# Four pairs of k instead of three by Strassen's products, in every second group of gates and ups

## The chip, the core and the metric

The kernel runs on one core of a Trainium2 chip. The metric is the time of one execution in device microseconds; the median of three runs is given, and beside it the profiler's record of one execution.

## What is computed

A decoder block for 256 positions of width 2048 in float32: a mixer (causal pooling and differential attention), and then a dense feed-forward part. The change lies in the feed-forward part alone:

```python
D_MODEL = 2048
D_FF = int(math.ceil(8 * D_MODEL / 3 / 256) * 256)   # 5632
...
hn = rms_norm(h, pre_ffn_norm[l])
ff = (jax.nn.silu(hn @ w_gate[l]) * (hn @ w_up[l])) @ w_down[l]
h = h + rms_norm(ff, post_ffn_norm[l])
```

## The kernel before

**Three matmuls for one product.** Every float32 operand is split in two parts: ScalarE copies it to a rounded part (named with h: `wh`, `rh`, `gh`), VectorE subtracts that from the operand and leaves the rest (named with l: `wl`, `rl`, `gl`). A product is then three matmuls: rounded by rounded, rest by rounded, rounded by rest. In `product` they stand in lines 768, 769 and 770; the first two read `wh`, the third is the first to read `wl`.

**Groups and pairs.** The 5632 columns of gate and up are 11 groups of 512. The first group is done apart. The other ten, c = 1 to 10, take gate and up together: k runs over 2048 rows in eight pairs (j = 0 to 7) of two blocks of 128 rows. For one pair there are four blocks of weights (two of k, by up and gate) and four blocks of h (two of k, by two halves of the positions). A plain pair multiplies them in 8 products, 24 matmuls of 128x512. A pair listed in `SK` takes Strassen's form (with Winograd's sums) of 7 products, 21 matmuls: three on single blocks of weights (`rh`, `rl`), and four on sums of blocks (`wh`, `wl` of the tile `T`). The sums of h for such a pair are the same for every group; `h_sums` makes them once, ahead of the ten groups, while the first group's ups run.

**What is done for one pair, q, and when.** `first_stage(q)` starts the two transfers of the four blocks into `raw` (three buffers in turn) and, in a Strassen pair, has VectorE make `T` (one buffer): one addition of 128x1024 and two of 128x512. `raw_stage(q)` splits three blocks into `rh` and `rl` (two buffers each) for a Strassen pair. `last_stage(q)` splits either `T` or `raw` into `wh` and `wl` (two buffers each), 128x2048. The loop over pairs runs `products(q)`, then `last_stage(q + 1)`, `first_stage(q + 2)` and `raw_stage(q + 2)`: while TensorE is at pair q, VectorE makes wl of the next pair, then T and rl of the one after it. Within a Strassen pair the order of products is 1, 3, 2 (on rh, rl: nine matmuls), then 7, 6, 4, 5 (on wh, wl). So its third matmul is the first to read `rl`, its twelfth the first to read `wl`.

**What sets the order.** Each of the three engines works its queue in the order written: `put` ties every matmul, copy and subtraction of this stage behind the one before it on its engine. Elsewhere a scheduler interleaves. Added to the pairs are the ends of the groups: behind pair 6 and behind pair 7 VectorE joins the products' sums (`u`, `sg`), behind pair 0 of the next group it multiplies gate and up (`gg`), and TensorE transposes the result (`g_part`).

Of the kernel before, what the change touches and what calls it, by code (L numbers as in the profile page):

```python
# [15 lines left out]
P = 128  # L16
# [13 lines left out]
H_GATE = {(0, 0): (0, 3), (0, 7): (1, 0), (0, 9): (1, 1), (0, 11): (1, 2), (1, 2): (1, 3)}  # L30
RING = 3
WINDOWS = (2, 4, 8, 16)
SK = (1, 3, 5)
CMB = 8


# [9 lines left out]
def block_kernel(ctx: ExitStack, tc: tile.TileContext, x, xT, pos, cols, rows, lamv, invf, invcnt,  # L46
# [4 lines left out]
    cp = ctx.enter_context(tc.tile_pool(name="cp", bufs=1))  # L51
# [8 lines left out]
    def nm(s):  # L60
        uid[0] += 1
        return f"{s}_{uid[0]}"

    def small(shape, dt=F32, tag="tiny", bufs=24):
        return tiny.tile(shape, dt, tag=tag, name=nm(tag), bufs=bufs)
# [20 lines left out]
    def load_after(dst, src):  # L86

        with tc.issue_after(latest[0]):
            sync.dma_start(dst, src)
# [51 lines left out]
    def gemm_a(srcs, a, nk, order=None, before=lambda i: None):  # L141
        ps = [bank(), bank()]
        for i, k, wh, wl in a_steps(srcs, order):
            before(i)
            for t in range(2):
                mm_a(ps, a, t, k, wh, wl, i == 0, i == nk - 1)
        return ps
# [127 lines left out]
    for k in range(NKD):  # L275
        n = 1 if k < 2 else 2
        i, j = k // 4, k % 4
# [5 lines left out]
        for m in range(2):  # L283
            raw, hi, lo = raws[m]
            c = slice(j % 2 * 512, (j % 2 + n) * 512)
# [3 lines left out]
        for m in range(2):  # L289
            raw, hi, lo = raws[m]  # L290
            if n == 1 or j % 2 == 0:
                c = slice(j % 2 * 512, (j % 2 + n) * 512)
                act.activation(hi[:, c], raw[:, c], AF.Copy)
                dve.tensor_tensor(lo[:, c], raw[:, c], hi[:, c].bitcast(F32), ALU.subtract)
            c = slice(j % 2 * 512, (j % 2 + 1) * 512)
# [237 lines left out]
    def closing(srcs_of, a, nk, gains, order, tail, parts, hook, done):  # L533

        sst = small([P, 2, 4], tag="sst", bufs=2)
        mg = {}

        def square(c, t, ps):
            j2 = cp.tile([P, 512], mybir.dt.bfloat16, tag="sqj", name=nm("sqj"), bufs=2)
            act.activation(j2, ps, AF.Square, accum_out=sst[:, t, c:c + 1])  # L540

        def gained(c, t, ps):
            mg[c, t] = mg_tile()
            dve.tensor_tensor(mg[c, t], ps, gain, ALU.mult)

        for c in range(4):
            if c == 1:
                act.activation(small([P, 1]), sst[:, 0, 0:1], AF.Sqrt)
            gain = cp.tile([P, 512], F32, tag="gain", name=nm("gain"), bufs=2)
            load_after(gain, gains[c * 512:(c + 1) * 512].partition_broadcast(P))  # L550
            if c < 3:
                ps = gemm_a(srcs_of(c), a, nk, order, lambda i: before_k[0](c, i))
                for t in range(2):
                    square(c, t, ps[t][:, :])
                    gained(c, t, ps[t][:, :])
        pre = small([P, 2])
        dve.tensor_reduce(pre, sst[:, :, 0:3], AX.X, ALU.add)
        pre2 = small([P, 2])
        dve.tensor_scalar(pre2, pre, 1.0 / D, EPS, ALU.mult, ALU.add)
        for t, ps in gemm_a_skew(srcs_of(3), a, nk, order, range(nk - tail, nk), parts, hook):  # L560
            square(3, t, ps[:, :])
            v = variance(sst[:, t, 3:4], 1.0 / D, pre2[:, t:t + 1])
            gained(3, t, ps[:, :])
            rs = rsqrt(v)
            for c in range(4):
                for z in (slice(0, 256), slice(256, 512)) if c == 0 and t == 1 else (slice(0, 512),):
                    dve.scalar_tensor_tensor(h_c(c, t)[:, z], mg[c, t][:, z], rs, h_c(c, t)[:, z], ALU.mult, ALU.add)
                    done(c, t, z)
# [31 lines left out]

    def h_stats(t):
        for c in range(4):
            j2 = cp.tile([P, 512], mybir.dt.bfloat16, tag="sqj", name=nm("sqj"), bufs=2)
            with tc.issue_after(behind_act[0]):
                act.activation(j2, h_c(c, t), AF.Square, accum_out=ss3[:, t, c:c + 1])
        ss3s = small([P, 1])
        dve.tensor_reduce(ss3s, ss3[:, t, :], AX.X, ALU.add)
        dve.tensor_copy(rstd3[:, t:t + 1], rsqrt(variance(ss3s, 1.0 / D)))
# [49 lines left out]
        sums_h[j], sums_l[j] = h, l  # L658


    h_at = dict(zip(range(2, 16, 4), SK))
    ps = gemm_a([w_u0[i] for i in range(4)], a_h, NKD, None, lambda i: h_sums(h_at[i]) if i in h_at else None)
    p_ring.close()
    ring2 = ctx.enter_context(tc.tile_pool(name="ring2", bufs=1, side="right", reuse_waits="tile"))
# [12 lines left out]
    def tt(out_, a, b, op):  # L677
        put("dve", lambda: dve.tensor_tensor(out_, a, b, op))  # L678
        return out_
# [37 lines left out]
    cmb = lambda name: ft.tile([P, 512], F32, tag="cmb", name=nm(name), bufs=CMB)  # L717

    NP = NKD // 2
    pairs = [(c, j) for c in range(1, NF // 4) for j in range(NP)]  # L720
    raws, sums, of_raw, of_sum = {}, {}, {}, {}

    def first_stage(q):

        if q >= len(pairs):
            return
        c, j = pairs[q]
        raws[q] = raw = blocks(w_gu[c - 1], j)
        if j in SK:
            sums[q] = s = part("T", 4, F32, 1)  # L730
            tt(s[:, 0:2], raw[:, 1:3], raw[:, 0:1].to_broadcast([P, 2, 512]), ALU.add)
            tt(s[:, 2], s[:, 0], raw[:, 2], ALU.add)
            tt(s[:, 3], s[:, 2], raw[:, 3], ALU.add)

    def raw_stage(q):

        if q < len(pairs) and pairs[q][1] in SK:
            rh = high(raws[q][:, 1:4], "rh")
            of_raw[q] = rh, low(raws[q][:, 1:4], rh, "rl")

# [20 lines left out]
    m, left, total, u = {}, {}, {}, {}  # L761
# [10 lines left out]
    def products(q):  # L772
        c, j = pairs[q]
        k1, k2 = 2 * j, 2 * j + 1
        if j == 0:
            m.update({1: bank(), 2: bank(), 3: bank(), 4: bank(), 6: bank2(), 8: bank2()})
            m[7] = psum_m.tile([P, 512], F32, tag="m7", name=nm("m7"), bufs=1)
            left.update({i: len(SK) + (2 * (NP - len(SK)) if i in (2, 3, 4) else 0) for i in range(1, 8)})
            left[8] = 2 * (NP - len(SK))
            total.update(left)  # L780
        wh, wl = of_sum[q]
        if j not in SK:
            for i, t, up in ((2, 0, 0), (4, 1, 0), (3, 0, 1), (8, 1, 1)):
                for k, b in ((k1, 1 - up), (k2, 3 - up)):
                    product(i, hh(k, t), wh[:, b], wl[:, b])
            return
        if j == SK[0]:
            m[5] = m5_bank()
        rh, rl = of_raw[q]
        form = lambda i: (sums_h[j][:, i], sums_l[j][:, i])  # L790
        product(1, hh(k1, 0), rh[:, 0], rl[:, 0])
        product(3, form(3), rh[:, 1], rl[:, 1])
        product(2, hh(k2, 0), rh[:, 2], rl[:, 2])
        product(7, form(1), wh[:, 1], wl[:, 1])
        product(6, form(2), wh[:, 2], wl[:, 2])
        product(4, hh(k2, 1), wh[:, 3], wl[:, 3])
        product(5, form(0), wh[:, 0], wl[:, 0])
# [5 lines left out]
    gg = [gated(ps[t][:, :], t) for t in range(2)]  # L803
    for q, (c, j) in enumerate(pairs):
        products(q)
        if j == SK[-1] + 1:
            u.update({n: cmb(f"u{n}") for n in (1, 2, 3, 4)})
            copy(u[1], m[1][:, :])
            tt(u[2], m[6][:, :], u[1], ALU.add)
            tt(u[3], m[7][:, :], u[2], ALU.add)  # L810
            last_stage(q + 1)
            tt(u[4], m[5][:, :], u[2], ALU.add)
            tt(u[2], m[5][:, :], u[3], ALU.add)
            first_stage(q + 2)
        elif j == NP - 1:
            last_stage(q + 1)
            sg = [cp.tile([P, 512], F32, tag="gain", name=nm("sg"), bufs=2) for _ in range(2)]
            for t, (i, n) in enumerate(((2, 1), (4, 3))):
                tt(sg[t], m[i][:, :], u[n], ALU.add)
                copy(sg[t], sg[t], AF.Silu, scale=rstd3[:, t:t + 1])  # L820
            first_stage(q + 2)
            for i, n in ((3, 4), (8, 2)):
                tt(u[n], m[i][:, :], u[n], ALU.subtract)
            raw_stage(q + 2)
            g_part(c - 1, gg, 0)
            if c == NF // 4 - 1:
                g_part(c - 1, gg, 1)
                g_split(0, gh0)
                gg = [gated(u[n], t) for t, n in enumerate((4, 2))]
        elif j == 0 and c > 1:  # L830
            last_stage(q + 1)
            new = [gated(u[n], t) for t, n in enumerate((4, 2))]
            first_stage(q + 2)
            raw_stage(q + 2)
            g_part(c - 2, gg, 1)
            gg = new
        else:
            last_stage(q + 1)
            first_stage(q + 2)
            raw_stage(q + 2)  # L840
# [40 lines left out]
    def mg_tile():  # L881
        n = len(mgs)
        if used[0] == n:
            three = part("rh" if n % 2 == 0 else "rl", 3, F32)
            mgs.extend(three[:, i] for i in range(3))
        used[0] += 1
        return mgs[used[0] - 1]
# [68 lines left out]
```

## Time and profile before

| | |
|---|---|
| median of three runs | 1024.69 us (1024.68 to 1025.0) |
| the profiled execution's own time | 1026.65 us |
| its span, first to last instruction | 1024.8 us |
| TensorE busy | 1012.2 us, 99% |
| VectorE busy | 735.5 us, 72% |
| ScalarE busy | 539.5 us, 53% |
| moved | 203.39 MB, 198 GB/s on the mean |

The profile gives busy times of each engine over the span, the same in 40 slices, the chain of work that ended last, followed back from the last instruction, and groups of like instructions. In a row of a timeline stand the start and the duration in us, the engine, the line of the kernel, the operation, output and inputs (buffer numbers left out), shapes, and in brackets the idle time of that engine just before it with what ended it. A window row gives, for a stretch of the span, its length, the busy time of TensorE's matmuls, of its weight loads, of VectorE, ScalarE and GpSimd, then TensorE's granted clock, the share of the DMA engines' time and GB/s. PE is TensorE, DVE is VectorE, ACT is ScalarE, SP the queue that starts the transfers. Matmuls are pipelined, so their rows overlap: the distance of starts is their price, not the duration.

### The profile page before, as it was taken

To read this page: it belongs to the slowest core of one execution; us is meant where nothing else is said; L and a number is where in the kernel's file an instruction comes from. 1 tells how busy PE (TensorE), PEld (TensorE's weight loads), DVE (VectorE), ACT (ScalarE), POOL (GpSimd) and SP (SyncE) were. 2 spreads that over 40 slices of the span, in tenths; PEclk is the share of its full clock that TensorE was granted. 3 is DMA by queue.
4 is the path that set the end of the run, shared out by engine and by line. 5 is a ranking of instruction groups with operands and counts; after the bars stand their busy time and mean duration, and the time that the engine had idled before them with its cause. 6 is when DMAs were issued, how large, how long until landed. Compare 5 with 4: busy or idle time off the path is not lost.

```text
span 1024.8 us, 12559 instructions
## 1 busy us (share of the span) xinstructions
PE 1012.2 (99%) x4787; PEld 841.7 (82%) x4787; DVE 735.5 (72%) x850; ACT 539.5 (53%) x643; POOL 28.4 (3%) x54
## 2 busy tenths in 40 slices
PE   9999999999999999999999999999999999999996
PEld 6889888988877888888888888888887888888885
DVE  6569755875677889898888988889887653454445
ACT  6666545654548555455454554645545553343332
POOL 0003300210000000000000000000000000000000
PEclk9999999999999999999999999999999999999999
DMA  9753555456774465555655556556565575556552
GB/s 337 284 191 131 180 186 177 151 169 217 237 255 135 165 228 192 199 201 194 206 197 195 202 185 205 206 201 200 174 211 189 196 287 198 191 196 216 181 189 82
DMA packets 57373, 203.39 MB, mean 198 GB/s; under 512 B 6880, under 2 KB 7520, under 8 KB 56544
## 3 DMA queue, kind: packets, MB, share of 16 engines
q1 hardware_dynamic: 57024, 202.44, 57.4%
q8 instruction: 37, 0.61, 0.2%
q14 instruction: 24, 0.20, 0.1%
q10 hardware_dynamic: 288, 0.15, 0.1%
HBM read 198.37 MB, written 4.19 MB: 198 GB/s over the span
## 4 chain that ended last, share of the span: by engine, by line
PE 98%; DVE 1%; DMA 0%; ACT 0%; issue 0%; DVEq 0%; SPq 0%; ACTq 0%
PE mm L136 16%; PE mm L137 16%; PE mm L135 16%; PE mm L768 9%; PE mm L769 9%; PE mm L770 9%; PE tr L770 3%; PE tr L769 3%; PE tr L768 3%; PE mm L174 2%; PE mm L175 2%; PE mm L176 2%; PE m L768 1%; PE m L769 1%; PE m L770 1%; PE m L692 1%
## 5 line engine op out<-in xcount | busy, mean ns | idle before, releaser
L100 DVE TENSOR_TENSOR wl<-raw,wh 128x1024 fp32r<-128x1024 f32 x88 | 104.7, 1222 | 107.6 <-ACT wh L99 107.6
L100 DVE TENSOR_TENSOR wlo<-raw,whi 128x1024 fp32r<-128x1024 f32 x89 | 110.5, 1241 | 61.9 <-ACT whi L99 56.5
L99 ACT ACTIVATE wh<-raw 128x1024 fp32r<-128x1024 f32 x88 | 89.3, 1052 | 122.4 <-PE mm L136 118.8
L678 DVE TENSOR_TENSOR wl<-raw,wh 128x2048 fp32r<-128x2048 f32 x50 | 114.6, 2292 | 44.0 <-ACT wh L674 43.7
L136 PE MATMUL mm<-wh,gl 128*128 128x512 f32 x352 | 137.3, 390 | 1.1 <-DVE gl L758 1.1
L674 ACT ACTIVATE wh<-raw 128x2048 fp32r<-128x2048 f32 x50 | 95.9, 1918 | 79.5 <-PE tr L769 56.4
L135 PE MATMUL mm<-wh,gh 128*128 128x512 f32 x352 | 134.9, 390 | 0.0
L137 PE MATMUL mm<-wl,gh 128*128 128x512 f32 x352 | 131.0, 389 | 0.0
L768 PE MATMUL mm<-wh,h 128*128 128x512 f32 x330 | 129.2, 392 | 0.0
L99 ACT ACTIVATE whi<-raw 128x1024 fp32r<-128x1024 f32 x89 | 94.0, 1056 | 65.7 <-PE mm L136 49.9
L769 PE MATMUL mm<-wh,h 128*128 128x512 f32 x330 | 128.5, 389 | 0.0
L770 PE MATMUL mm<-wl,h 128*128 128x512 f32 x330 | 128.4, 389 | 0.0
L674 ACT ACTIVATE wh<-T 128x2048 fp32r<-128x2048 f32 x30 | 57.6, 1920 | 73.8 <-DVE T L678 73.4
L136 PEld LDWEIGHTS mm<-wh,gl 128*128 128x128 f32 x352 | 66.1, 188 | 15.1 <-DVE gl L758 1.6
L137 PEld LDWEIGHTS mm<-wl,gh 128*128 128x128 f32 x352 | 66.1, 188 | 13.7
L135 PEld LDWEIGHTS mm<-wh,gh 128*128 128x128 f32 x352 | 66.0, 188 | 13.6
L678 DVE TENSOR_TENSOR wl<-T,wh 128x2048 fp32r<-128x2048 f32 x30 | 68.7, 2290 | 8.0 <-ACT wh L674 8.0
L770 PEld LDWEIGHTS mm<-wl,h 128*128 128x128 f32 x330 | 62.0, 188 | 12.9
L768 PEld LDWEIGHTS mm<-wh,h 128*128 128x128 f32 x330 | 62.0, 188 | 12.7
L769 PEld LDWEIGHTS mm<-wh,h 128*128 128x128 f32 x330 | 62.0, 188 | 12.5
L135 PE MATMUL mm<-whi,x 128*128 128x512 f32 x160 | 62.9, 395 | 0.6 <-ACT x L255 0.6
L136 PE MATMUL mm<-whi,x 128*128 128x512 f32 x160 | 62.8, 394 | 0.0
(246 smaller groups left out, 1941.3 us busy)
## 6 DMA issues: line engine op xcount, KB each, us to landing
raw<-in_w_gu SPq DMA_DIRECT2D x160, 512.0 KB, 4.2
raw<-in_w_down SPq DMA_DIRECT2D x88, 512.0 KB, 4.1
raw<-in_w_in SPq DMA_DIRECT2D x46, 512.0 KB, 3.8
raw<-in_w_out SPq DMA_DIRECT2D x32, 512.0 KB, 4.2
raw<-in_w_u SPq DMA_DIRECT2D x24, 512.0 KB, 3.7
raw<-in_w_g SPq DMA_DIRECT2D x8, 512.0 KB, 6.1
xn<-in_x SPq DMA_DIRECT2D x2, 1024.0 KB, 10.1
gain<-in_rows SPq DMA_DIRECT2D x8, 256.0 KB, 4.6
```

The costliest lines, as they stand in the source:

```text
L99: last_split[0] = act.activation(hi, raw, AF.Copy).ins
L100: (by or dve).tensor_tensor(lo, raw, hi.bitcast(F32), ALU.subtract)
L135: mm.matmul(ps[t][:, :], lhsT=a[0](k, t), rhs=wh, start=first, stop=False)
L136: mm.matmul(ps[t][:, :], lhsT=a[1](k, t), rhs=wh, start=False, stop=False)
L137: last_mm[0] = mm.matmul(ps[t][:, :], lhsT=a[0](k, t), rhs=wl, start=False, stop=last).ins
L174: mm.matmul(o, lhsT=wh, rhs=xh, start=st, stop=False)
L175: mm.matmul(o, lhsT=wh, rhs=xl, start=False, stop=False)
L674: put("act", lambda: act.activation(out_, in_, func, **kw))
L678: put("dve", lambda: dve.tensor_tensor(out_, a, b, op))
L768: put("mm", lambda: mm.matmul(o, lhsT=a[0], rhs=wh, start=first, stop=False))
L769: put("mm", lambda: mm.matmul(o, lhsT=a[1], rhs=wh, start=False, stop=False))
L770: put("mm", lambda: mm.matmul(o, lhsT=a[0], rhs=wl, start=False, stop=last))
```

## The change

Every second group (c = 2, 4, 6, 8, 10) takes pairs 1, 2, 3 and 5 in Strassen's form instead of 1, 3 and 5; the others stay. `h_sums` is called four times, at steps 2, 5, 8 and 11 of the first group's ups instead of three times at 2, 6 and 10. The scratch tile `sqj`, into which ScalarE writes squares of which only the sums are used, has one buffer instead of two.

```diff
-SK = (1, 3, 5)
+SKS = ((1, 3, 5), (1, 2, 3, 5))
...
-            j2 = cp.tile([P, 512], mybir.dt.bfloat16, tag="sqj", name=nm("sqj"), bufs=2)
+            j2 = cp.tile([P, 512], mybir.dt.bfloat16, tag="sqj", name=nm("sqj"), bufs=1)
...
-    h_at = dict(zip(range(2, 16, 4), SK))
+    h_at = dict(zip(range(2, 14, 3), SKS[1]))
...
+    sk = lambda c: SKS[(c + 1) % 2]
...
-        if j in SK:
+        if j in sk(c):
             sums[q] = s = part("T", 4, F32, 1)
             tt(s[:, 0:2], raw[:, 1:3], raw[:, 0:1].to_broadcast([P, 2, 512]), ALU.add)
             tt(s[:, 2], s[:, 0], raw[:, 2], ALU.add)
             tt(s[:, 3], s[:, 2], raw[:, 3], ALU.add)
...
-        if q < len(pairs) and pairs[q][1] in SK:
+        if q < len(pairs) and pairs[q][1] in sk(pairs[q][0]):
             rh = high(raws[q][:, 1:4], "rh")
             of_raw[q] = rh, low(raws[q][:, 1:4], rh, "rl")
...
-            left.update({i: len(SK) + (2 * (NP - len(SK)) if i in (2, 3, 4) else 0) for i in range(1, 8)})
-            left[8] = 2 * (NP - len(SK))
+            n = len(sk(c))
+            left.update({i: n + (2 * (NP - n) if i in (2, 3, 4) else 0) for i in range(1, 8)})
+            left[8] = 2 * (NP - n)
...
-        if j not in SK:
+        if j not in sk(c):
...
-        if j == SK[0]:
+        if j == sk(c)[0]:
             m[5] = m5_bank()
...
-        if j == SK[-1] + 1:
+        if j == sk(c)[-1] + 1:
```

VectorE's queue in the group c = 2, from rl and wl of pair 1 to wl of pair 3 or 4. Before:

```order
L678 TENSOR_TENSOR rl_3822<-raw_3811,rh_3820 128x1536
L678 TENSOR_TENSOR wl_3863<-T_3814,wh_3861 128x2048
L683 SCALAR_TENSOR_TENSOR gg_3865<-u_746_3764,rstd_2330,sg_3805 128x512
L683 SCALAR_TENSOR_TENSOR gg_3867<-u_744_3762,rstd_2330,sg_3806 128x512
L678 TENSOR_TENSOR wl_3902<-raw_3869,wh_3900 128x2048
L678 TENSOR_TENSOR T_3907<-raw_3904 128x1024
L678 TENSOR_TENSOR T_3907<-T_3907,raw_3904 128x512 x2
L678 TENSOR_TENSOR rl_3913<-raw_3904,rh_3911 128x1536
L678 TENSOR_TENSOR wl_3941<-T_3907,wh_3939 128x2048
```

And now:

```order
L678 TENSOR_TENSOR rl_3835<-raw_3824,rh_3833 128x1536
L678 TENSOR_TENSOR wl_3876<-T_3827,wh_3874 128x2048
L683 SCALAR_TENSOR_TENSOR gg_3878<-u_748_3777,rstd_2330,sg_3818 128x512
L683 SCALAR_TENSOR_TENSOR gg_3880<-u_746_3775,rstd_2330,sg_3819 128x512
L678 TENSOR_TENSOR T_3885<-raw_3882 128x1024
L678 TENSOR_TENSOR T_3885<-T_3885,raw_3882 128x512 x2
L678 TENSOR_TENSOR rl_3891<-raw_3882,rh_3889 128x1536
L678 TENSOR_TENSOR wl_3923<-T_3885,wh_3921 128x2048
L678 TENSOR_TENSOR T_3928<-raw_3925 128x1024
L678 TENSOR_TENSOR T_3928<-T_3928,raw_3925 128x512 x2
L678 TENSOR_TENSOR rl_3934<-raw_3925,rh_3932 128x1536
L678 TENSOR_TENSOR wl_3959<-T_3928,wh_3957 128x2048
```

Between gg and wl of pair 2 now stand its T (three additions) and its rl, and wl reads T in place of raw; pair 3 follows as before.

TensorE's queue at the same place, the first matmuls of pair 2. Before:

```order
L768 MATMUL mm_3831<-wh_3900,h_2309 128x512
L769 MATMUL mm_3831<-wh_3900,h_2309 128x512
L770 MATMUL mm_3831<-wl_3902,h_2309 128x512
L768 MATMUL mm_3831<-wh_3900,h_2310 128x512
L769 MATMUL mm_3831<-wh_3900,h_2310 128x512
L770 MATMUL mm_3831<-wl_3902,h_2310 128x512
```

And now (the file has one line more above, so `product` stands at 769 to 771):

```order
L769 MATMUL mm_3843<-rh_3889,h_2309 128x512
L770 MATMUL mm_3843<-rh_3889,h_2309 128x512
L771 MATMUL mm_3843<-rl_3891,h_2309 128x512
L769 MATMUL mm_3845<-rh_3889,sh_3394 128x512
L770 MATMUL mm_3845<-rh_3889,sl_3401 128x512
L771 MATMUL mm_3845<-rl_3891,sh_3394 128x512
L769 MATMUL mm_3844<-rh_3889,h_2310 128x512
L770 MATMUL mm_3844<-rh_3889,h_2310 128x512
L771 MATMUL mm_3844<-rl_3891,h_2310 128x512
L769 MATMUL m_767_3849<-wh_3921,sh_3394 128x512
L770 MATMUL m_767_3849<-wh_3921,sl_3401 128x512
L771 MATMUL m_767_3849<-wl_3923,sh_3394 128x512
```

The first matmul on a subtracted part is the third in both, wl of `raw` before, rl now; the first on T's parts, wh and wl, are the tenth and the twelfth.

VectorE's queue at the end of the first group's ups (`wlo` are the rests of their weights, `sl` the rests of the sums of h), up to the first pair's wl. Before:

```order
L100 TENSOR_TENSOR wlo_3446<-raw_3427,whi_3445 128x1024
L653 TENSOR_TENSOR hs_3452<-hf_3449,hs_3452 128x128
L657 TENSOR_TENSOR sl_3362<-hs_3354,sh_3355 128x512
L657 TENSOR_TENSOR sl_3411<-hs_3403,sh_3404 128x512
L654 TENSOR_SCALAR hs_3452<-hs_3452 128x128
L100 TENSOR_TENSOR wlo_3479<-raw_3474,whi_3478 128x1024
L657 TENSOR_TENSOR sl_3460<-hs_3452,sh_3453 128x512
L100 TENSOR_TENSOR wlo_3495<-raw_3476,whi_3494 128x1024
L678 TENSOR_TENSOR wl_3519<-raw_3514,wh_3517 128x2048
```

And now:

```order
L652 TENSOR_TENSOR hs_3471<-hf_3468,hs_3471 128x128
L608 COPY rstd_2330<-tiny_3290 128x1
L100 TENSOR_TENSOR wlo_3492<-raw_3487,whi_3491 128x1024
L654 TENSOR_SCALAR hs_3436<-hs_3436 128x128
L657 TENSOR_TENSOR sl_3401<-hs_3393,sh_3394 128x512
L653 TENSOR_TENSOR hs_3471<-hf_3468,hs_3471 128x128
L100 TENSOR_TENSOR wlo_3508<-raw_3489,whi_3507 128x1024
L654 TENSOR_SCALAR hs_3471<-hs_3471 128x128
L657 TENSOR_TENSOR sl_3444<-hs_3436,sh_3437 128x512
L657 TENSOR_TENSOR sl_3479<-hs_3471,sh_3472 128x512
L678 TENSOR_TENSOR wl_3532<-raw_3527,wh_3530 128x2048
```

Between the last weights of the ups and the first wl now stand the last two sums' rests and one scaling of a sum (L654); the rest of the fourth set is spread over the rows ahead.

More of the change, by code (lines that the diff above doesn't have):

```diff
@@ L602, in h_stats @@
         for c in range(4):
-            j2 = cp.tile([P, 512], mybir.dt.bfloat16, tag="sqj", name=nm("sqj"), bufs=2)
+            j2 = cp.tile([P, 512], mybir.dt.bfloat16, tag="sqj", name=nm("sqj"), bufs=1)
             with tc.issue_after(behind_act[0]):
```

## Prediction

> **What bounds the kernel now.** I read the page first (busy times, slices, chain of waits), then the windows of two stages, then the timeline of one group of gates and ups.
>
> ```profile
> span 1024.8 us, 12559 instructions
> PE 1012.2 (99%) x4787; PEld 841.7 (82%) x4787; DVE 735.5 (72%) x850; ACT 539.5 (53%) x643; POOL 28.4 (3%) x54
> DVE  6569755875677889898888988889887653454445
> PE 98%; DVE 1%; DMA 0%; ACT 0%; issue 0%; DVEq 0%; SPq 0%; ACTq 0%
> ...
> 326.00:350.00 24.00, 24.00 (x108) 19.88 (x106) 20.77 (x47) 18.19 (x22) 0.00 (x0) 1.00 0.33 110
> 392.30:434.75 42.45, 42.45 (x193) 35.14 (x192) 37.12 (x31) 23.30 (x19) 0.00 (x0) 1.00 0.58 199
> 774.00:778.00 4.00, 2.86 (x15) 2.08 (x13) 4.00 (x6) 3.28 (x5) 0.00 (x0) 1.00 0.87 281
> ```
>
> TensorE carries 98% of the chain, so fewer matmuls should be less time. But VectorE's slices stand at 8 and 9 in the stage of the gates and ups, and the second window, one group of eight pairs (here c=2, 42.45 us), shows TensorE without a gap and VectorE busy for 37.12 us: 5.33 us free, on an engine that the change loads. Where those 5.33 us lie decides.
>
> ```profile
> 388.19 2.29 DVE L678 TENSOR_TENSOR wl<-raw,wh 128x2048 fp32r<-128x2048 f32 x1 [1.82 <-ACT wh L674]
> 397.05 2.28 DVE L678 TENSOR_TENSOR wl<-T,wh 128x2048 fp32r<-128x2048 f32 x1
> 399.25 1.41 DVE L683 SCALAR_TENSOR_TENSOR gg<-u,rstd,sg 128x512 f32<-128x512 f32 x2
> 400.69 2.29 DVE L678 TENSOR_TENSOR wl<-raw,wh 128x2048 fp32r<-128x2048 f32 x1
> 402.90 1.22 DVE L678 TENSOR_TENSOR T<-raw 128x1024 f32<-128x1024 f32 x1
> 404.15 1.42 DVE L678 TENSOR_TENSOR T<-T,raw 128x512 f32<-128x512 f32 x2
> 405.49 1.75 DVE L678 TENSOR_TENSOR rl<-raw,rh 128x1536 fp32r<-128x1536 f32 x1
> 407.62 2.29 DVE L678 TENSOR_TENSOR wl<-T,wh 128x2048 fp32r<-128x2048 f32 x1 [0.38 <-ACT wh L674]
> 410.28 2.29 DVE L678 TENSOR_TENSOR wl<-raw,wh 128x2048 fp32r<-128x2048 f32 x1 [0.37 <-ACT wh L674]
> ...
> 405.66 1.92 ACT L674 ACTIVATE wh<-T 128x2048 fp32r<-128x2048 f32 x1 [2.60 <-DVE T L678]
> 418.53 1.92 ACT L674 ACTIVATE wh<-raw 128x2048 fp32r<-128x2048 f32 x1 [1.33 <-PE tr L769]
> ...
> 402.87 0.39 PE L768 MATMUL mm<-wh,h 128*128 128x512 f32 x1
> 403.32 0.39 PE L770 MATMUL mm<-wl,h 128*128 128x512 f32 x1
> 408.31 0.39 PE L768 MATMUL mm<-rh,h 128*128 128x512 f32 x1
> 413.07 0.39 PE L768 MATMUL mm<-wh,h 128*128 128x512 f32 x1
> 418.51 0.39 PE L768 MATMUL mm<-rh,h 128*128 128x512 f32 x1
> ```
>
> The first fence is VectorE in this group. The bracket is idle time before an instruction: from 388.19, where the end of the previous group is worked off, to 407.62 there is none. The last is TensorE: the first matmuls of pairs 2, 3, 4 and 5 start at 402.87, 408.31, 413.07 and 418.51, the third of pair 2 at 403.32. From 408.31 to 418.51 are 21 + 24 matmuls, so one per 0.227 us; the 0.39 us in a row overlap.
>
> **The change, part by part.**
>
> *Removed matmuls.* A plain pair has 8 products of 3 matmuls, a Strassen pair 7. Five groups (c = 2, 4, 6, 8, 10) turn pair 2: 5 x 3 x 0.227 = 3.4 us less on TensorE, all of it on the chain.
>
> *Added VectorE work.* Pair 2 now needs T (three additions) and rl ahead of its wl. From T's start to rl's end before: 405.49 + 1.75 - 402.90 = 4.34 us, against 5.33 us free in a group. On average it fits. In place it does not: pairs 1, 2 and 3 now stand side by side, each asks 4.34 us for T and rl and 2.2 us for wl, 6.5 us, of VectorE while TensorE needs 21 x 0.227 = 4.77 us for the one before, and the run without idle time ends in just these pairs.
>
> *Pair 2 by these rows.* T starts where wl did, at 400.69 (gg ahead of it is unchanged). rl starts 2.59 us behind T (405.49 - 402.90), at 403.28, and ends at 405.03. TensorE wants it for its third matmul at 403.32, and its queue stands. How a wait ends is shown where the down stage begins:
>
> ```profile
> 775.20 0.69 DVE gl L758
> ...
> 775.94 0.50 PE L136 MATMUL mm<-wh,gl 128*128 128x512 f32 x1 [1.14 <-DVE gl L758]
> 776.27 0.40 PE L137 MATMUL mm<-wl,gh 128*128 128x512 f32 x1
> ```
>
> The matmul starts 0.05 us behind the producer's end, and the one after it 0.33 us later, not 0.227. So the third matmul goes at 405.08, 1.76 us late. The twelfth, the first to read wl, would come 0.33 + 8 x 0.227 later, at 407.23. wl starts 4.72 us behind T (407.62 - 402.90; ScalarE's wh of T stands between, 405.66 in the rows, 0.09 us behind T's end) at 405.41 and ends at 407.70: second wait, 0.52 us, to 407.75. Ten steps, 0.33 + 9 x 0.227 = 2.38 us, bring pair 3 to 410.13. Without waits it were 402.87 + 4.77 = 407.64: 2.5 us lost.
>
> *Pair 3.* T has one buffer, so its T waits until wl has read pair 2's: 407.70 + 0.03 (the gap between dependent additions, 402.90 + 1.22 to 404.15) = 407.73. rl is done at 407.73 + 4.34 = 412.07; the third matmul is due at 410.13 + 0.45 = 410.58 and goes at 412.12, 1.54 us late. The twelfth could go at 414.27; wl runs from 407.73 + 4.72 = 412.45 to 414.74, so it goes at 414.79, 0.52 us late. Pair 4 starts at 414.79 + 2.38 = 417.17. Before it was 413.07: **4.1 us later per group**, the three removed matmuls counted in.
>
> *Pairs 4 to 7.* wl of pair 4 follows at 414.66 and is done at 416.95, in time. T of pair 5 starts at about 416.9, its rl ends at 421.2; pair 5's third matmul comes at 417.17 + 24 x 0.227 + 0.45 = 423.06. From there ScalarE's wh of pair 6 is released by TensorE, as at 418.53 before, and all runs in the old distances, shifted by 4.1 us. The next group has three pairs and the old pattern: nothing is caught up, nothing is added. Five groups: 20.5 us.
>
> *Transfers.* raw has three buffers, and pair 5's transfer is released by the end of pair 2's reading.
>
> ```profile
> 403.01 0.80 SPq L707 DMA_DIRECT2D raw<-in_w_gu  x2
> raw<-in_w_gu SPq DMA_DIRECT2D x160, 512.0 KB, 4.2
> ```
>
> It was issued at 403.01, behind wl; now behind rl at 405.03. With 4.2 us to land each, and two, it is there by about 411, and T of pair 5 asks at 416.9: nothing. SP's order is unchanged.
>
> *The fourth set of sums of h* (h_sums) runs on VectorE in the first ups, L646 to L657.
>
> ```profile
> L646 DVE TENSOR_TENSOR hf<-h 128x256 f32<-128x256 f32 x6 | 2.4, 418 | 0.0
> L650 DVE TENSOR_TENSOR hs<-hf 128x128 f32<-128x128 f32 x3 | 0.9, 285 | 0.0
> L654 DVE TENSOR_SCALAR hs<-hs 128x128 f32<-128x128 f32 x3 | 0.7, 220 | 0.0
> L657 DVE TENSOR_TENSOR sl<-hs,sh 128x512 fp32r<-128x512 f32 x3 | 2.0, 686 | 0.0
> ...
> 345.19 2.29 DVE L678 TENSOR_TENSOR wl<-raw,wh 128x2048 fp32r<-128x2048 f32 x1 [0.31 <-ACT wh L674]
> 350.68 0.39 PE L770 MATMUL mm<-wl,h 128*128 128x512 f32 x1
> ```
>
> 2 x 0.418 + 4 x 0.285 + 0.220 + 0.686 = 2.9 us. That window leaves VectorE 24.00 - 20.77 = 3.2 us free, and behind it the first wl ends at 347.48 while TensorE asks at 350.68, 3.2 us of slack. Each alone covers it: I take 0, at most 1 us if the new order of the rows costs more. The single buffer of sqj adds a wait of ScalarE on itself, for an instruction long finished: 0.
>
> *Sum.* 1024.8 + 20.5 = 1045.3 us by the span; the profiled execution itself took 1026.65, the median of the runs is 1024.69. Against the median: **1045.2 us**. Bounds: if neither wait on wl came about, because ScalarE's wh ran sooner than these rows have it, pair 3's rl would still hold TensorE to 412.12, its twelfth matmul would go at 414.27, pair 4 at 416.65, 3.6 us a group: 17.9, and 1042.6. If each of the six handovers in the chain T, wh, wl, T, wh, wl, matmul took 0.15 us more (the 0.38 us idle ahead of wl shows that such steps are not free), 5.0 us a group: 25, and 1049.7. I stay with the rows' own distances.
>
> **A rule weighed.** The waits could cost TensorE its clock.
>
> ```profile
> core 0: 1024.8 us, clock 0.998
> ...
> 8.32 0.63 PE L136 MATMUL mm<-whi,x 128*128 128x512 f32 x1
> 8.75 0.63 PE L137 MATMUL mm<-wlo,x 128*128 128x512 f32 x1
> ```
>
> Only the start runs slowly (0.43 us from matmul to matmul), and after the idle 1.14 us at 774.8 the window shows 1.00. The Trainium skill, "TensorE: Matmul & The Clock Gate", section "HAM oscillation — how this bites in real kernels", says that gaps up to about 3.4 us leave the clock alone; my longest is 1.76 us, so by that rule too the sum stands. Its section "A second HAM failure mode: psum-queue depth-cycling" says that frequent short idling can make the clock swing; by that the sum would be that of the fourth rival. No row here has two waits of this size within 10 us.
>
> **The rivals.**
> - *Faster: VectorE is ahead after all.* If T of pair 2 began 1.7 us earlier (rl by 403.32) and pair 3's as well, no matmul would wait, and the 3.4 us are gained: 1021.3 us. For it speak the 5.33 us free per group; against it that none lies between 388.19 and 407.62, and that T cannot be drawn ahead of gg. Chance 0.04, and 0.01 for something in between that ends within 0.2%, about what a measurement of this kernel can tell from no change.
> - *Only one of the two pairs waits:* if VectorE made up during the first wait, a group would lose 2.5 - 0.7 = 1.8 us: 1033.8. Against it: T's single buffer ties pair 3 to pair 2's wl. Chance 0.07.
> - *The lateness lasts.* Pair 5's rl has 1.85 us to spare (421.2 to 423.06), pair 6's wl 0.9 (by the old distances done at 418.53 + 1.92 + 2.29 = 422.74, asked for at 418.51 + 4.77 + 0.45 = 423.73). If raw of pair 5 lands later or handovers add up past these, another wait comes: 1 us to 2 us a group, about 1052. Chance 0.10.
> - *The clock swings.* 1 - 0.998 of 1024.8 is 2 us for one slow phase; one for each of the ten pairs that wait adds 20.5: 1066. Chance 0.04.
>
> **How the numbers follow.** The forecast itself has 0.74, its own range 1042.6 to 1049.7. The range has to leave out at most 2 in 10: the faster cases (0.05), the single wait (0.07) and the clock (0.04) are left out with it, the lasting lateness half taken in: 1041 to 1051. Faster 0.04, within 0.2% 0.01, slower 0.95.
>
> **What would show it.** Right: in c=2, 4, 6, 8, 10 TensorE waits on VectorE four times, near 1.76, 0.52, 1.54 and 0.52 us, at the third and twelfth matmuls of pairs 2 and 3; groups of 46.5 and 42.45 us in turn; idle time of VectorE only behind pair 4; granted clock 0.998; no new wait between 326 and 358 us. Wrong: TensorE without gaps in these groups, waits on ScalarE or on raw in place of VectorE, waits in pairs 5 to 7, or a lower clock.

## Result: slower, and the profile after

The changed kernel took 1049.69 us (median of five, 1048.32 to 1051.49) against 1025.0 us of the kernel before in the same comparison: a ratio of 1.0232, 95% interval 1.022 to 1.0243. The profiled execution took 1049.69 us with a span of 1047.9 us, 23.1 us over the span before.

The page of the kernel after: busy times, VectorE's slices, the chain.

```profile
span 1047.9 us, 12581 instructions
PE 1015.2 (97%) x4772; PEld 836.6 (80%) x4772; DVE 758.7 (72%) x878; ACT 547.1 (52%) x649; POOL 28.5 (3%) x54
DVE  6559746865777779898888988989897664444544
PE 80%; DVE 12%; ACT 4%; issue 2%; DMA 0%; DVEq 0%; SPq 0%; ACTq 0%
```

VectorE's share of the span is 72% as before, but VectorE and ScalarE now hold 16% of the chain that ended last. The busy times would not have told it. The waits of TensorE do; a row gives the sum in us, the number of waits and the longest:

```profile
PE mm L771 <- DVE rl L678: 14.1, 10, 1.5
PE m L771 <- DVE wl L678: 3.2, 10, 0.3
PE mm L769 <- DVE gg L683: 2.3, 1, 2.3
```

Ten waits on rl and ten on wl are two each in five groups, as forecast. The third line is one that was not. In the group c = 2 (VectorE, then TensorE):

```profile
400.03 2.28 DVE L678 TENSOR_TENSOR wl<-T,wh 128x2048 fp32r<-128x2048 f32 x1
402.23 1.41 DVE L683 SCALAR_TENSOR_TENSOR gg<-u,rstd,sg 128x512 f32<-128x512 f32 x2
403.55 1.22 DVE L678 TENSOR_TENSOR T<-raw 128x1024 f32<-128x1024 f32 x1
406.14 1.75 DVE L678 TENSOR_TENSOR rl<-raw,rh 128x1536 fp32r<-128x1536 f32 x1
408.20 2.29 DVE L678 TENSOR_TENSOR wl<-T,wh 128x2048 fp32r<-128x2048 f32 x1 [0.31 <-ACT wh L674]
410.53 1.22 DVE L678 TENSOR_TENSOR T<-raw 128x1024 f32<-128x1024 f32 x1
413.13 1.75 DVE L678 TENSOR_TENSOR rl<-raw,rh 128x1536 fp32r<-128x1536 f32 x1
415.25 2.29 DVE L678 TENSOR_TENSOR wl<-T,wh 128x2048 fp32r<-128x2048 f32 x1 [0.37 <-ACT wh L674]
...
406.08 0.39 PE L770 MATMUL mm<-rh,h 128*128 128x512 f32 x1
407.95 0.50 PE L771 MATMUL mm<-rl,h 128*128 128x512 f32 x1 [1.48 <-DVE rl L678]
410.55 0.50 PE L771 MATMUL m<-wl,sh 128*128 128x512 f32 x1 [0.27 <-DVE wl L678]
414.93 0.50 PE L771 MATMUL mm<-rl,h 128*128 128x512 f32 x1 [1.37 <-DVE rl L678]
417.59 0.50 PE L771 MATMUL m<-wl,sh 128*128 128x512 f32 x1 [0.33 <-DVE wl L678]
```

rl of pair 2 ends at 406.14 + 1.75 = 407.89 and its matmul starts at 407.95, 1.87 us behind the one before it where 0.227 would do: 1.64 us late (the bracket counts from the modelled end of the matmul before, so it reads less). T of pair 3 stands at 410.53, behind wl at 408.20, and so on. In the chain the start of the wl of pair 0, from group c = 2 to group c = 10:

```profile
391.17 1.03 DVE wl L678
746.75 1.03 DVE wl L678
```

Eight groups took 355.58 us; eight of before take 8 x 42.45 = 339.6. Four of the eight are changed, so a changed group is 4.0 us longer (forecast 4.1). The fifth, c = 10, is no different: from its gg to the first gl of the down stage are 40.40 us, and 36.38 before. The five cost 20.0 us. In front of them, wl of pair 0 of c = 2 starts at 391.17, at 388.19 before: 2.98 us. Together 23.0 of the 23.1 us.

Those 2.98 us come from the first pair, c = 1, pair 0. Before, then after:

```profile
351.65 1.40 DVE L683 SCALAR_TENSOR_TENSOR gg<-mm,rstd,sg 128x512 f32<-128x512 f32 x2
352.94 0.39 PE L768 MATMUL mm<-wh,h 128*128 128x512 f32 x1
```

```profile
348.57 0.39 PE L769 MATMUL mm<-wh,h 128*128 128x512 f32 x1
351.49 0.40 PE L771 MATMUL mm<-wl,h 128*128 128x512 f32 x1
353.43 1.40 DVE L683 SCALAR_TENSOR_TENSOR gg<-mm,rstd,sg 128x512 f32<-128x512 f32 x2
354.23 0.80 PE L769 MATMUL mm<-wh,h 128*128 128x512 f32 x1 [2.34 <-DVE gg L683]
355.25 0.63 PE L771 MATMUL mm<-wl,h 128*128 128x512 f32 x1
355.68 0.63 PE L769 MATMUL mm<-wh,h 128*128 128x512 f32 x1
```

The thirteenth matmul of this pair writes a PSUM bank that held the ups of the first group, which VectorE's gg reads. Before, the first of the two gg was done at about 352.4 and the matmul came at 352.94: half a us to spare. Now gg comes 1.8 us later, and TensorE, which reached the pair sooner (348.57 against 350.22), stands for 2.5 us. Even the first wl, which had 3.2 us of slack before, now ends at 349.25, and the third matmul of the pair starts 0.28 us late for it, at 349.31.

Why VectorE is late, before (ScalarE) and after (VectorE, then ScalarE):

```profile
343.25 1.91 ACT L674 ACTIVATE wh<-raw 128x2048 fp32r<-128x2048 f32 x1
```

```profile
344.24 0.22 DVE L654 TENSOR_SCALAR hs<-hs 128x128 f32<-128x128 f32 x1
344.37 1.48 DVE L657 TENSOR_TENSOR sl<-hs,sh 128x512 fp32r<-128x512 f32 x2
346.96 2.29 DVE L678 TENSOR_TENSOR wl<-raw,wh 128x2048 fp32r<-128x2048 f32 x1 [1.11 <-ACT wh L674]
...
344.49 0.63 ACT L655 ACTIVATE sh<-hs 128x512 fp32r<-128x512 f32 x1 [0.91 <-DVE hs L654]
345.03 1.90 ACT L674 ACTIVATE wh<-raw 128x2048 fp32r<-128x2048 f32 x1
```

VectorE is not busy right up to the first wl; it stands idle for 1.11 us, because ScalarE's wh comes late. In ScalarE's queue wh stands behind `sh`, the rounded copy of the last set of sums, and that copy waited for VectorE's scaling of the sum (L654). So wh starts 1.78 us later than before, and with it wl and all that follows on VectorE, gg included.

Not all of the shift between the two engines is the fourth set's. From the pair's first matmul to gg are 1.43 us before and 4.86 now. In the kernel with the groups alone (below), which makes three sets as before, it is 2.51 us already (348.16 to 350.67). It has the single buffer of `sqj` in common with the changed kernel; no run changes that alone, so where this 1.1 us comes from is not shown.

Behind the gap TensorE's matmuls start 0.43 us apart instead of 0.227. A window row there:

```profile
355.50:357.00 1.50, 1.50 (x5) 1.12 (x5) 1.50 (x1) 0.00 (x0) 0.00 (x0) 0.50 0.92 350
```

The granted clock was 0.50. The twelve matmuls from 354.23 took 4.39 us instead of 2.72.

### The profile page after: what moved, and what is told of

Same layout as the page of the kernel before. It is cut to its first block, busy times and chain, and to the rows that moved or that the text cites. A ratio compares the mean times of both kernels' runs of the same rounds, so it can differ in the third digit from the quotient of the medians.

```text
span 1047.9 us, 12581 instructions
## 1 busy us (share of the span) xinstructions
PE 1015.2 (97%) x4772; PEld 836.6 (80%) x4772; DVE 758.7 (72%) x878; ACT 547.1 (52%) x649; POOL 28.5 (3%) x54
## 4 chain that ended last, share of the span: by engine, by line
PE 80%; DVE 12%; ACT 4%; issue 2%; DMA 0%; DVEq 0%; SPq 0%; ACTq 0%
PE mm L136 14%; PE mm L137 14%; PE mm L135 14%; PE mm L769 6%; PE mm L770 6%; PE mm L771 6%; DVE T L678 4%; DVE wl L678 4%; ACT wh L674 3%; PE tr L769 2%; PE tr L770 2%; PE tr L771 2%; PE mm L174 2%; PE mm L175 1%; PE mm L176 1%
## 5 line engine op out<-in xcount | busy, mean ns | idle before, releaser
L678 DVE TENSOR_TENSOR wl<-raw,wh 128x2048 fp32r<-128x2048 f32 x45 | 103.1, 2292 | 42.9 <-ACT wh L674 42.7
L674 ACT ACTIVATE wh<-raw 128x2048 fp32r<-128x2048 f32 x45 | 86.3, 1917 | 75.9 <-PE tr L770 52.8
L769 PE MATMUL mm<-wh,h 128*128 128x512 f32 x305 | 120.2, 394 | 2.3 <-DVE gg L683 2.3
L674 ACT ACTIVATE wh<-T 128x2048 fp32r<-128x2048 f32 x35 | 67.1, 1917 | 100.8 <-DVE T L678 100.4
L771 PE MATMUL mm<-wl,h 128*128 128x512 f32 x305 | 119.3, 391 | 0.1
L770 PE MATMUL mm<-wh,h 128*128 128x512 f32 x305 | 119.3, 391 | 0.0
L678 DVE TENSOR_TENSOR wl<-T,wh 128x2048 fp32r<-128x2048 f32 x35 | 80.1, 2290 | 9.7 <-ACT wh L674 9.7
L769 PEld LDWEIGHTS mm<-wh,h 128*128 128x128 f32 x305 | 57.5, 189 | 14.5 <-DVE gg L683 2.8
L771 PEld LDWEIGHTS mm<-wl,h 128*128 128x128 f32 x305 | 57.5, 189 | 12.6 <-DVE wl L678 0.5
L770 PEld LDWEIGHTS mm<-wh,h 128*128 128x128 f32 x305 | 57.6, 189 | 11.7
```

Source lines behind the costliest of these rows:

```text
L674: put("act", lambda: act.activation(out_, in_, func, **kw))
L769: put("mm", lambda: mm.matmul(o, lhsT=a[0], rhs=wh, start=first, stop=False))
L770: put("mm", lambda: mm.matmul(o, lhsT=a[1], rhs=wh, start=False, stop=False))
L771: put("mm", lambda: mm.matmul(o, lhsT=a[0], rhs=wl, start=False, stop=last))
```

## Experiments

Times over before are worked out from the ratio of each comparison and 1025 us. The edits are against the changed kernel, or against another one where that is said.

**The head alone.**

```diff
-SKS = ((1, 3, 5), (1, 2, 3, 5))
+SKS = ((1, 3, 5), (1, 3, 5))
-    h_at = dict(zip(range(2, 14, 3), SKS[1]))
+    h_at = dict(zip(range(2, 14, 3), (1, 2, 3, 5)))
```

> The groups of the kernel before (pairs 1, 3, 5 in all ten), with the four sets of sums of h of the changed kernel ahead of them; the fourth set is made and never read. Theory A (the fourth set delays gg on VectorE, and the first pair's matmuls wait for the PSUM bank that gg reads): one wait of TensorE on gg near 2.3 us at about 352 us, then some matmuls 0.43 us apart, in all 2.5 to 4 us over before, 1027.5 to 1029. Theory B (the prediction's step: VectorE's free 3.2 us hide it): 0 to 0.3 us, no wait on gg.

Measured: ratio 1.0027 (1.0014 to 1.0039), 2.8 us over before; span 1027.7 against 1024.8.

```profile
PE mm L769 <- DVE gg L683: 2.3, 1, 2.3
```

Theory A, but for one part: the clock stayed at 1.00 here. The gap is the same 2.5 us, and the matmuls 0.43 us apart that were expected behind it did not come. TensorE reaches the pair at 349.90 us, only 0.3 us sooner than before, so the gap alone costs what in the changed kernel gap, slow clock and a start 1.65 us sooner make together.

**The groups alone.** The sums for pair 2 are taken out of the first group's ups and tied into VectorE's queue in group 1. `h_sums_late` (not printed) does the same steps as `h_sums`, each tied behind the one before it.

```diff
-    h_at = dict(zip(range(2, 14, 3), SKS[1]))
+    h_at = dict(zip(range(2, 16, 4), SKS[0]))
...
             last_stage(q + 1)
+            if q == 5:
+                h_sums_late(2)
             first_stage(q + 2)
```

> The groups of the changed kernel, but the sums of h for pair 2 are made in group 1, behind wl of pair 6, so that the first group's ups have three sets as before. Theory A (two separate prices, groups and head): no wait on gg, the four waits of every second group as in the changed kernel, 5 x 3.9 = 19.7 us over before, 1044 to 1045.5. Theory B (the head's delay makes the groups' waits, or the two overlap): the time of the changed kernel, 1048 to 1050, or well under 19 us over before.

Measured: ratio 1.0206 (1.0191 to 1.0221), 21.1 us; span 1044.3, 19.5 us over before's. The waits:

```profile
PE mm L771 <- DVE rl L678: 13.8, 10, 1.5
PE m L771 <- DVE wl L678: 3.2, 10, 0.4
PE mm L769 <- DVE gg L683: 0.4, 1, 0.4
```

Theory A: the waits in the groups are those of the changed kernel, and the two parts add up: 1.0027 and 1.0206 against 1.0232. The wait on gg is not quite gone (0.4 us), though three sets are made as before: the half a us to spare did not cover the 1.1 us told above. And 0.8 us went to a wait on wl next to the late sums.

**The same work, placed otherwise.** Two kernels with three Strassen pairs in every group, as many matmuls and as much VectorE work as before; the edits are against the kernel before.

```diff
-SK = (1, 3, 5)
+SK = (1, 2, 4)
```

> The kernel before with pairs 1, 2, 4 in Strassen's form in all ten groups in place of 1, 3, 5: same matmuls, same work for VectorE and ScalarE in each group, three sets of sums. Theory A (place decides: T and rl of pair 2 fall into the stretch in which VectorE has no idle time): waits on rl (about 1.5 to 1.8 us) and wl (0.3 to 0.5 us) at pair 2 of nine groups, about 2.3 us each, 19 to 23 us over before, 1044 to 1048. Theory B (VectorE's total work in a group decides): no difference, 1024 to 1026.

Measured: ratio 1.0218 (1.0203 to 1.0233), 22.3 us.

```profile
PE mm L770 <- DVE rl L678: 13.3, 9, 1.5
PE m L770 <- DVE wl L678: 2.7, 9, 0.3
```

```diff
-SK = (1, 3, 5)
+SK = (1, 4, 5)
```

> The kernel before with pairs 1, 4, 5 in Strassen's form in all ten groups: again the same matmuls and the same work, two Strassen pairs side by side, but later in the group, where VectorE has idle time ahead of them. Theory A (place decides): by the rows of before rl of pair 5 is there 0.6 us ahead of its matmul and wl just in time, so 0 to 3 us over before. Theory C (two Strassen pairs side by side always cost, since T has one buffer): waits at pair 5 of ten groups of about 2.3 us, 20 to 24 us over before.

Measured: ratio 1.0023 (1.0013 to 1.0033), 2.4 us. No wait of TensorE on VectorE is listed in its groups, but they are a little longer. VectorE has rl of pair 1 in the groups c = 2 and c = 3, and between them wl of pair 5; TensorE's chain has the first matmul on that wl:

```profile
395.37 1.75 DVE L678 TENSOR_TENSOR rl<-raw,rh 128x1536 fp32r<-128x1536 f32 x1
418.83 2.29 DVE L678 TENSOR_TENSOR wl<-T,wh 128x2048 fp32r<-128x2048 f32 x1 [0.40 <-ACT wh L674]
438.13 1.75 DVE L678 TENSOR_TENSOR rl<-raw,rh 128x1536 fp32r<-128x1536 f32 x1
...
421.18 0.50 PE m L770
```

42.76 us instead of 42.45, 0.3 us a group. It is a wait too short to be listed: wl ends at 421.12, its matmul starts 0.06 us behind that, 0.39 us behind the matmul ahead of it, and the next one 0.33 us later. So theory A: VectorE's total work in a group does not decide, and neither do two Strassen pairs side by side by themselves. Two such pairs cost 2.4 us a group (44.85 us from gg to gg, in nine groups) in the stretch without idle time and 0.3 us where 1.8 us of idle time stand ahead of them.

**T's additions on GpSimd.** From the kernel with the groups alone; T gets two buffers.

```diff
-            sums[q] = s = part("T", 4, F32, 1)
-            tt(s[:, 0:2], raw[:, 1:3], raw[:, 0:1].to_broadcast([P, 2, 512]), ALU.add)
+            sums[q] = s = part("T", 4, F32, 2)
+            add = (lambda *a: put("pool", lambda: pool.tensor_tensor(*a))) if j in (2, 3) and len(sk(c)) > 3 else tt
+            add(s[:, 0:2], raw[:, 1:3], raw[:, 0:1].to_broadcast([P, 2, 512]), ALU.add)
...
-CMB = 8
+CMB = 4
```

> Four pairs in every second group as in the changed kernel, sums of h of pair 2 made in group 1, but the three additions of T of pairs 2 and 3 run on GpSimd, T has two buffers (and the ring that holds u four buffers in place of eight to make room). VectorE then does rl and wl alone for these pairs. Theory A (the additions on VectorE, in a stretch without idle time, are what makes TensorE wait): rl of pair 2 about 1 us ahead of its matmul, no waits in these groups, and the 15 removed matmuls come through: 3.4 us under before, if GpSimd makes a T within about 6 us (its additions of 256 elements took 0.6 to 1.5 us before, so 5 to 12 us for 2048; above some 7 us wl of pair 3 is late again and the gain goes). Theory B (rl and wl themselves, or ScalarE's parts, keep TensorE waiting): still 10 us or more over before.

Measured: ratio 1.034 (1.032 to 1.036), 35 us over before. By the time it is theory B's case (10 us or more), but its reason is not what the rows show: a third thing happened. GpSimd, then VectorE, then TensorE:

```profile
395.44 3.33 POOL L732 TENSOR_TENSOR T<-T,raw 128x512 f32<-128x512 f32 x2
402.81 2.82 POOL L732 TENSOR_TENSOR T<-raw 128x1024 f32<-128x1024 f32 x1 [4.04 <-DVE wl L678]
...
393.13 4.48 DVE L678 TENSOR_TENSOR T<-T,raw 128x512 f32<-128x512 f32 x2
402.60 3.58 DVE L683 SCALAR_TENSOR_TENSOR gg<-u,rstd,sg 128x512 f32<-128x512 f32 x2
406.10 2.81 DVE L678 TENSOR_TENSOR rl<-raw,rh 128x1536 fp32r<-128x1536 f32 x1
...
408.97 0.80 PE L772 MATMUL mm<-rl,h 128*128 128x512 f32 x1 [3.18 <-DVE rl L678]
```

While GpSimd works, VectorE's two additions take 4.48 us (1.42 before), gg 3.58 (1.41), rl 2.81 (1.75). In the next group of the same run, where GpSimd does nothing, they take 1.42, 1.41 and 1.75 us again. So what was taken off VectorE's queue came back as longer instructions in the same place. This run therefore does not tell whether a shorter queue would help; the run with gg moved does.

**The same in nine groups.**

```diff
-    sk = lambda c: SKS[(c + 1) % 2]
+    sk = lambda c: SKS[c > 1]
```

> As the run with T of pairs 2 and 3 on GpSimd, but four pairs in all groups from c = 2 on, nine groups: 27 matmuls fewer than before. Theory A: 27 x 0.227 = 6.1 us under before, if GpSimd keeps up. Theory B: twice the loss of that run.

Measured: ratio 1.0596 (1.0575 to 1.0616), 61 us: theory B, roughly. Nine groups cost 1.75 times what five did, and the mean granted clock fell to 0.977.

**Two buffers for T, on VectorE.** Again from the kernel with the groups alone.

```diff
-            sums[q] = s = part("T", 4, F32, 1)
+            sums[q] = s = part("T", 4, F32, 2)
...
-CMB = 8
+CMB = 4
```

> The kernel with the changed groups and the head of before (sums of h of pair 2 made in group 1), T on VectorE as there, but with two buffers for T (ring of u with four buffers to make room). Theory A (VectorE's queue, in which T of pair 3 stands behind wl of pair 2, sets the waits, not T's buffer): same as the run with one buffer within 1 us, four waits in each of five groups. Theory C (T's one buffer ties pair 3): the waits at pair 3 go, some 9 us less.

Measured: ratio 1.0217 (1.0201 to 1.0234), 22.2 us, not to be told from 21.1; the waits:

```profile
PE mm L771 <- DVE rl L678: 13.1, 10, 1.5
PE m L771 <- DVE wl L678: 3.2, 10, 0.4
```

Theory A: T's buffer is not what ties pair 3 to pair 2. VectorE's queue is: T of pair 3 stands behind wl of pair 2 whatever it may write to.

**A shorter queue ahead of the same pairs.** From the kernel with the groups alone, gg is moved from ahead of T of pair 2 to behind wl of pair 6.

```diff
         elif j == 0 and c > 1:
             last_stage(q + 1)
-            new = [gated(u[n], t) for t, n in enumerate((4, 2))]
             first_stage(q + 2)
             raw_stage(q + 2)
             g_part(c - 2, gg, 1)
-            gg = new
         else:
             last_stage(q + 1)
+            if j == 5 and c > 1:
+                gg = [gated(u[n], t) for t, n in enumerate((4, 2))]
```

> The changed groups with the head of before (as in the run on groups only), and gg, the two multiplications of gate and up that stand ahead of T of pair 2 on VectorE, moved behind wl of pair 6 in all groups; nobody reads gg before pair 7 is done. Theory A (the length of VectorE's queue ahead of rl and wl sets the waits): everything from T of pair 2 on comes 1.4 us sooner, the wait on rl of pair 2 shrinks from about 1.5 to under 0.3 us, the other three stay, 1.4 us less in each of five groups: 7 us under the run on groups only, 12 to 15 us over before. Theory B (handovers between VectorE, ScalarE and TensorE set them): as the run on groups only, 20 to 22 us over before.

Measured: ratio 1.015 (1.0134 to 1.0165), 15.4 us, 5.7 us less than the groups alone.

```profile
PE mm L771 <- DVE rl L678: 7.9, 9, 1.4
PE m L771 <- DVE wl L678: 3.2, 10, 0.3
```

The waits on rl fall from 13.8 to 7.9 us, those of pair 2 to 0.3 us at most, and the waits on wl stay, as theory A has it; the 5.7 us is a little under its 7, and 15.4 us just above its 12 to 15. Nothing but the queue's order was changed, so the length of VectorE's queue ahead of rl is shown to set that wait.

**gg first in the head.** From the kernel with the head alone.

```diff
+    gg = [gated(ps[t][:, :], t) for t in range(2)]
     first_stage(1)
     raw_stage(1)
-    gg = [gated(ps[t][:, :], t) for t in range(2)]
```

> As the run on the head only (groups of before, four sets of sums of h in the first group's ups), with gg of the first group ahead of T of pair 1 on VectorE. Theory A (the head's price is the PSUM bank that gg releases late): no wait on gg near 352 us, at most 0.7 us of waits at pair 1, 0 to 0.8 us over before. Theory B (the price is the later weights and parts themselves): as the run on the head only, 2.5 to 3 us over before.

Measured: ratio 1.0002 (0.9994 to 1.0011). The head's price is gone with the order of three steps, though VectorE's first wl is as late as in the kernel with the head alone (idle for 1.11 us ahead of it). What is left in the groups' stage is one line:

```profile
PE m L771 <- DVE wl L678: 0.3, 1, 0.3
```

Theory A: what cost the time was the bank that gg frees late. No version with four pairs came out under the kernel before. The best of them, gg moved and the head as before, is 15.4 us over it; with pairs 2 and 3 still fed through one VectorE queue, their wl waits and pair 3's rl wait remain.

## Why the prediction was right, and where a term was off

The direction and the place were right. The five groups' term was 20.5 us; the trace has 20.0, and the kernel with the groups alone 19.5 by the span, 21.1 (19.6 to 22.7) by the ratio. Step by step in c = 2:

| | forecast | trace |
|---|---|---|
| end of rl of pair 2 behind T's start | 4.34 us | 4.34 us |
| its matmul late | 1.76 us | 1.64 us |
| matmul on wl of pair 2 late (410.55, due at 410.12) | 0.52 us | 0.43 us |
| T of pair 3 behind T of pair 2 | 7.04 us | 6.98 us |
| matmuls on rl and wl of pair 3 late | 1.54 and 0.52 us | 1.52 and 0.48 us |
| a changed group longer by | 4.1 us | 4.0 us |
| three-pair groups, gg to gg | 42.45 us | 42.45 us |
| later pairs | nothing | no further wait listed |

The saving of 3.4 us on TensorE is in that sum, and is real, but in these groups TensorE no longer sets the end.

**The term that was mis-sized is the head.** The prediction took 0, at most 1 us, for the fourth set of sums, because VectorE had 3.2 us free in that window and the first wl had 3.2 us of slack. It cost 2.98 us in the trace and 2.8 us (1.4 to 4.0) alone. Two things were missed, and a third is open. The 3.2 us of free time were a sum over the window and did not hide the set: the last set goes from VectorE to ScalarE and back (scaling, `sh`, then wh and wl of the first pair), and VectorE came out 1.8 us late although it stood idle for 1.11 us of that time. The slack was read at the one instruction next in the queue; the tight one stood four rows further back, gg, which frees a PSUM bank and had half a us. Open is the 1.1 us by which TensorE came nearer with three sets too: the one thing known that differs up to there is the single buffer of `sqj`, which the prediction took at 0 because the instruction waited for is long finished, and no run tests that. The run with gg first shows that the wait on gg was the price of the head. To take the 3.2 us as cover was the same error which the prediction warned of for the groups: free time on average but not in place.

**What was luck.** The profiled span rose by 23.1 us where 20.5 were forecast: 3.0 us for the head, 0.5 us less for the groups. The median came out 4.5 us over the forecast; the rest of that lies within the spread of executions (the kernel before took 1024.68 to 1027.33 us in the same comparison). That 1049.69 us lies inside the stated range is in part luck: its upper end was drawn from slower handovers in the groups and from lateness in later pairs, and neither came, while the head, which did, had no part in it.

The rivals: that TensorE would not wait and that only pair 2 would wait are refuted by the rows above; lateness past pair 4 is not listed. The clock did fall, but once, behind the gap in the head, and not behind the ten pairs of waits (1.00 in the windows over the groups). So two of the prediction's own signs went against it, both in the head: a new wait between 326 and 358 us, and a mean clock of 0.996. The prediction's own reason why pair 3 waits, T's single buffer, is refuted: with two buffers the waits are the same, and the queue's order is enough. Two slips changed nothing: pair 6's wl had 0.99 us to spare by the prediction's numbers, not 0.9, and its lower bound keeps rl of pair 3 in place though the sooner wl that it assumes would let T of pair 3 start sooner.

## What to carry to other kernels

Free time of an engine is worth something only between the wait that ends last and the instruction that comes too late; sum the queue between these two, not the stage. When work is put into a strictly ordered queue, walk every later instruction of that queue until its idle time has taken up the delay, and ask of each what it releases: operands, and also the buffers and PSUM banks that it reads last. Where the work passes through another engine, its queue is walked too: here the delay came through ScalarE. An engine at 87% in a group (37.12 of 42.45 us) whose idle time lies elsewhere is full.

## What the runs showed of the hardware

- VectorE slows down while GpSimd adds float32 tiles from SBUF: a VectorE addition of 128x512 rose from 0.71 to about 2.2 us. GpSimd took 2.85 us for 128x1024 and 1.99 us for each 128x512 on the mean; no run has it add these tiles alone, so whether it slows too is not shown. The Trainium skill, "SBUF — State Buffer", section "Who interferes with whom", says that a VectorE instruction with two SBUF inputs contends with a GpSimd instruction that reads SBUF; the trace agrees.
- A gap of 2.5 us on TensorE was followed by about 3 us at half clock in one kernel's profile and by none in another's, at the same place. The Trainium skill, "TensorE: Matmul & The Clock Gate", section "HAM oscillation — how this bites in real kernels", sets the gap that matters at about 3.4 us; in the first of these the measurement differs, and decides. In the two kernels with additions on GpSimd, matmuls 0.43 us apart followed 13 of the 14 gaps that are listed with 3.2 us, and none of the 14 that are listed with 1.1 to 1.5 us. What decides in between is open.
- After a wait the second matmul starts 0.33 us behind the first, not 0.227, here as in the kernel before.
